# A ten-stage transformer block: norm roots moved to GpSimd, and the causal convolution as 128x32 products

## The chip, the cores and the metric

The kernel runs on one core of a Trainium2 chip. The metric is the time of one execution in microseconds (us) of device time, as a median over runs. The engines are TensorE (PE; its weight loads are listed apart as PEld), VectorE (DVE), ScalarE (ACT), GpSimd (POOL) and SyncE (SP), whose queue issues nearly all transfers here.

## The reference, cut to what matters

Batch 1, 256 rows, width 1024, float32. Ten stages follow each other on the same residual `x`: a gated feed-forward net (F1), a mixer with convolution and windowed attention ("even"), F3, F4, forgetting attention ("fox"), F6, an mLSTM mixer ("ml"), F8, attention with relative positions ("rel"), F10, and a last norm. Every stage begins with an RMS norm of `x`; the first six also norm their result before it is added.

```python
def _rmsnorm(x, g):
    y = x * rsqrt(mean(x * x, axis=-1) + EPS)
    return y * g

def _conv_module(u, gate, w, b, ln_g, ln_b):      # u, gate: (256, 512)
    a = u * sigmoid(gate)
    y[t, c] = sum(a[t - 30 + j, c] * w[j, c] for j in range(31)) + b[c]
    y = layernorm(y) * ln_g + ln_b
    return silu(y)

h = concat([_conv_module(...), window_attention(...)]) @ w_out     # the even mixer
x = x + _rmsnorm(h, g3)
```

## The kernel before, in words

The 256 rows are two blocks of 128, b0 and b1. Every large product runs in the reduced type fp32r three times: each operand is split into a high part `hi` (an ACT copy) and a low part `lo` (a DVE subtraction), and `mm3` (line 673) adds hi·hi, hi·lo and lo·hi. The weights come as "units" of 128 x 2048 (two transfers of 512 KB), are split into tiles `hl`, and are used by both blocks. So the bulk of DVE's work are subtractions `hl<-b,hl` (`tt`, line 220, recorded as L223), the bulk of ACT's are copies `hl<-b` (L213), and the bulk of PE's are products of 512 columns (`mm`, line 280, recorded as L293; transposes are L298).

The order of the work is not that of the code. Every helper only records an operation with an engine, an estimated duration and a key (where in the sequence of units it belongs; block b1 lies `lead` = 4 units behind b0). `schedule` (line 319) then plays the engines' queues through with these estimates and hands out the buffers, and the instructions are emitted in the order of the starts that it finds. A table NUDGE (line 1732) shifts the keys of some 970 labelled groups by fixed amounts. Each engine then runs its own queue in order.

**The norms' roots.** `rstd` (line 579) takes sums of squares that ACT left in a column and makes 1/sqrt by VectorE alone: a first guess from the bits, three Newton steps, all on tiles `s` of 128x1 (or 128x4 for the mLSTM heads). For a norm at the start of a stage (`norm`, line 662, which also wants halves of the root) these are 12 instructions, for one at the end (`postnorm`, line 714) 10. `postnorm` squares the two halves of the result by ACT, multiplies them by the gain (DVE, L242 `b<-acc,g`), takes the root, and updates `x` (DVE, L242 `x<-b,s,x`); the next stage's `gain_T` (line 634) then multiplies `x` by the next gain (DVE, L223 `b<-x,g`) and transposes (L298). There are 20 roots at starts, 12 at ends, 2 in the convolution's layernorm, 4 for the mLSTM heads. The last norm (`final`, line 1620) alone already takes its root by GpSimd (`pow`, line 267): one TENSOR_SCALAR (L271) and one TENSOR_TENSOR with power -1/2 (L273).

**The convolution** (`even`, line 1260). The gated input is transposed to channels x time (four tiles `ct` of 128 channels; tile `aT`, with 30 zero columns ahead). Of the 4 x 31 taps, `cg` = 6 groups of 8 go to TensorE: all 31 taps of ct 0 and 15 of ct 1, for each block a product with a 128x128 diagonal matrix that is loaded (`in_diag`), 2 x 46 = 92 products of 128 columns in full float32. The trace shows a float32 product as two matmuls:

```python
for q in range(4 - ng[ct], 4):
    n = min(8, 31 - 8 * q)
    d = r.t("b4", n * P, name="diag")
    r.load(d[:, :], self.a["diag"][ct][:, q * 1024:q * 1024 + n * P], ...)
    for j in range(n):
        r.mm(bank[:, 0:P], d[:, j * P:(j + 1) * P], tap(ct, b * P + 8 * q + j, P), ...)
```

The other 78 taps run on VectorE, each one multiply-add over 128x256 (L242 `b<-aT,cst,b`). Then follow the layernorm, its transposes and the silu; in the output projection the convolution's channels come last (`order=(2, 3, 0, 1)`).

Buffers: `b4` (nine of 128x1024; raw weights, `y`, the diagonals, scores), `b2` (eleven of 128x512), `s` (sixteen), `aT` (four), and four PSUM banks `mm` and four `acc`.

Of the kernel before, what the change touches and what calls it, by code (L numbers as in the profile page):

```python
# [12 lines left out]
P = 128  # L13
# [63 lines left out]
class Rec:  # L77
# [13 lines left out]
    def alloc(self, ctx):  # L91
        for tag, (dt, cols, n, psum) in self.tags.items():
            kw = dict(space=(None, bass.MemoryType.PSUM, bass.MemoryType.DRAM)[psum]) if psum else {}
            pool = ctx.enter_context(self.tc.tile_pool(name="p_" + tag, bufs=1, **kw))
            rows = 16 if psum == 2 else P
            self.phys[tag] = [pool.tile([rows, cols], dt, tag=f"{tag}{i}", name=f"{tag}{i}") for i in range(n)]
# [170 lines left out]
    def pow(self, s, a, b, key=None):  # L267

        v, y, e = s[:, 0:1], s[:, 1:2], s[:, 2:3]
        self.op("POOL", 350, [a, b], [v],  # L270
                lambda: self.nc.gpsimd.tensor_scalar(self.res(v), self.res(a), self.res(b), EPS, ALU.add, ALU.add), key=key)  # L271
        self.op("POOL", 600, [v, e], [y],
                lambda: self.nc.gpsimd.tensor_tensor(self.res(y), self.res(v), self.res(e), ALU.pow), key=key)  # L273
        return y
# [25 lines left out]
    def load(self, out, src, nbytes, key=None, after=None):  # L300
        o = self.op("DMA", max(nbytes / (360.0 if key > 0 else 250.0), 453.0), [src], [out],
# [187 lines left out]
class Net:  # L489
# [12 lines left out]
    def consts(self):  # L502
# [3 lines left out]
        w = r.t("s", name="warm")  # L506
        r.memset(w[:, 0:1], 0.0, key=-40)
# [6 lines left out]
        for b in range(2):  # L514
            x = r.t("x", name=f"x{b}")
            for h in range(2):
                r.load(x[:, h * 512:(h + 1) * 512], a["x"][b * P:(b + 1) * P, h * 512:(h + 1) * 512], P * 2048, key=-30 + 0.15 * b + 0.75 * h)
# [61 lines left out]
    def rstd(self, ss, w, n, key, more=False, cut=1):  # L579
# [3 lines left out]
        v, vh, y, t = s[:, 0:w], s[:, w:2 * w], s[:, 2 * w:3 * w], s[:, 3 * w:4 * w]  # L583
        r.begin()
        r.ts(v, ss[0], 1.0 / n, EPS, ALU.mult, ALU.add)
        if len(ss) > 1:
            r.end(key)
            r.begin()
            r.stt(v, ss[1], 1.0 / n, v, ALU.mult, ALU.add)
        r.ts(y.bitcast(I32), v.bitcast(I32), -0.5, 1597463007.0, ALU.mult, ALU.add)  # L590
        r.ts(vh, v, -0.5, None, ALU.mult)
        for i in range(3):
            if w == 1:
                r.stt(t, y, vh, y, ALU.mult, ALU.mult)
            else:
                r.tt(t, y, y, ALU.mult)
                r.tt(t, t, vh, ALU.mult)
            r.stt(y, t, 1.5, y, ALU.add, ALU.mult)
            if cut > 1 and i < 2:
                r.end(key)  # L600
                r.begin()
        if more:
            r.stt(s[:, 5:6], y, 0.5, y, ALU.mult, ALU.mult)
            r.ts(s[:, 4:5], y, 0.5, None, ALU.mult)
        r.end(key)
        if more:
            return y, s[:, 4:5], s[:, 5:6]
# [17 lines left out]
    def ssq(self, b, key):  # L625
# [3 lines left out]
        for h in range(2):  # L629
            junk = r.t("b2", name="junk")  # L630
            r.act(junk[:, :], self.x[b][:, h * 512:(h + 1) * 512], AF.Square, accum=ss[:, h:h + 1], key=key)
# [82 lines left out]
    def postnorm(self, b, acc, g, scale):  # L714
# [5 lines left out]
        for h in range(2):  # L720
            sl = slice(h * 512, h * 512 + 512)
            junk = r.t("b2", name="junk")
            r.act(junk[:, :], acc[h][:, :], AF.Square, accum=ss[:, h:h + 1], key=key)
# [185 lines left out]
    def attn_group(self, b, key, qT, kT, v, bias, sgn, O, oc, den, sink=None, nd=2):  # L909
# [5 lines left out]
        sc = r.t("b4" if nk == 2 else "b2", name="sc")  # L915
# [146 lines left out]
    def fox(self, gi):  # L1062
# [51 lines left out]
        for b in range(2):  # L1114
            den.append(r.t("s", name="den"))
            vv[b] = r.t("b4", name="v")
        for j in range(4):
            for b in range(2):
# [15 lines left out]
                C = r.t("b4" if b else "b2", name="C")  # L1134
# [33 lines left out]
    def rel(self):  # L1168
# [19 lines left out]
        for b in range(2):  # L1188
# [15 lines left out]
            vv[b] = r.t("b4", name="v")  # L1204
# [55 lines left out]
    def even(self, gi):  # L1260
# [12 lines left out]
        cw, cbi, lg, lb = c[:, 520:644], c[:, 644:648], c[:, 648:652], c[:, 652:656]  # L1273
# [3 lines left out]
        T2 = 30 + 2 * P  # L1277
        a2 = [r.t("aT", 2 * T2, name="aT") for _ in range(2)]
        y = r.t("b4", name="yT")
        ng = [min(4, max(0, int(self.c["cg"]) - 4 * ct)) for ct in range(4)]  # L1280
        part = [None, None]

        def tap(ct, t0, n):
            o = (ct % 2) * T2 + t0
            return a2[ct // 2][:, o:o + n]

        for b in range(2):
# [14 lines left out]
            for i in range(2):  # L1302
                if b == 0:
                    r.begin()
                    for ct in (2 * i, 2 * i + 1):
                        r.memset(tap(ct, 0, 30), 0.0)
                    r.end(key)
                r.begin()
                for ct in (2 * i, 2 * i + 1):
                    r.copy(tap(ct, 30 + b * P, P), pt[:, ct * P:(ct + 1) * P])  # L1310
                r.end(key)
            r.lab = f"even conv b{b}"
            kp = self.pos(b, u0 + 3) - self.c["vp"]
            for ct in range(4):
                if ng[ct] == 0:
                    continue
                bank = r.t("mm", name="cv")
                for q in range(4 - ng[ct], 4):
                    n = min(8, 31 - 8 * q)
                    d = r.t("b4", n * P, name="diag")  # L1320
                    at = u0 + self.c["lead"] * b + self.c["du"] + 4 * ct + q
                    r.load(d[:, :], self.a["diag"][ct][:, q * 1024:q * 1024 + n * P], P * P * 4 * n, key=at, after=self.near(at))
                    r.begin()
                    for j in range(n):
                        r.mm(bank[:, 0:P], d[:, j * P:(j + 1) * P], tap(ct, b * P + 8 * q + j, P), q == 4 - ng[ct] and j == 0, q == 3 and j == n - 1)
                    r.end(kp)
                ys = y[:, (2 * ct + b) * P:(2 * ct + b + 1) * P]
                if ng[ct] == 4:
                    r.act(ys, bank[:, 0:P], AF.Identity, bias=cbi[:, ct:ct + 1], key=kp)
                else:  # L1330
                    part[b] = r.t("b1", name="part")
                    r.act(part[b][:, 0:P], bank[:, 0:P], AF.Copy, key=kp)
        r.lab = "even conv"
        key = self.pos(1, u0 + 3) - self.c["vb"]
        for j in range(31):
            r.begin()
            for ct in range(3, -1, -1):
                if j >= 8 * (4 - ng[ct]):
                    continue
                ys = y[:, 2 * ct * P:2 * (ct + 1) * P]  # L1340
                w = cw[:, ct * 31 + j:ct * 31 + j + 1]
                if j == 0:
                    r.ts(ys, tap(ct, j, 2 * P), w, cbi[:, ct:ct + 1], ALU.mult, ALU.add)
                else:
                    r.stt(ys, tap(ct, j, 2 * P), w, ys, ALU.mult, ALU.add)
            r.end(key)
        for ct in range(4):
            if 0 < ng[ct] < 4:
                for b in range(2):
                    ys = y[:, (2 * ct + b) * P:(2 * ct + b + 1) * P]  # L1350
                    r.tt(ys, part[b][:, 0:P], ys, ALU.add, key=key)
# [586 lines left out]
```

## Time and profile before

| what | us |
|---|---|
| median of 3 runs (lowest, highest) | 1586.29 (1584.86, 1587.45) |
| the profiled execution | 1587.08 |
| its span, first to last instruction | 1585.3 |
| TensorE busy | 1548.6 |
| VectorE busy | 1217.4 |
| ScalarE busy | 938.1 |
| GpSimd busy | 1.9 |

A group's row reads: line, engine, operation, out<-in by the program's names (buffer numbers left out), shapes, count | busy us, mean ns of one | idle time of the engine just before them and what ended it. In a timeline a row begins with the start and the duration of a run of like instructions. Matmuls overlap each other in the array, so the pace of a stream is read from starts, not from the mean of one.

### The profile page before, as it was taken

How to read it: one execution, taken by the hardware profiler on the slowest of the kernel's cores; microseconds unless marked ns; L12 is line 12 of the kernel's file. 1: busy time of each engine (PE TensorE's matmuls, PEld its weight loads, DVE VectorE, ACT ScalarE, POOL GpSimd, SP SyncE). 2: the span in 40 equal slices, each digit the busy share in tenths (PEclk: the TensorE clock that was granted, in tenths of full speed). 3: DMA queues.
4: the chain of work that ended last, by engine and by line, in shares of the span. 5: the costliest groups of instructions: out<-in, count | busy, mean ns of one | idle time of the engine just before them, and what ended most of it. 6: DMA issues, size and time to landing. Idle time of an engine off the chain costs nothing.

```text
span 1585.3 us, 21242 instructions
## 1 busy us (share of the span) xinstructions
PE 1548.6 (98%) x7546; PEld 1266.6 (80%) x7546; DVE 1217.4 (77%) x2137; ACT 938.1 (59%) x1480; POOL 1.9 (0%) x8
## 2 busy tenths in 40 slices
PE   8999999999999999999999999999999999999998
PEld 6888878788887888787787887788877887788886
DVE  6555689798878869776899687898788674788784
ACT  6444545865555656456875565656566566765562
POOL 0000000000000000000000000000000000000000
PEclk9999999999999999999999999999999999999999
DMA  8556466447474475643664475455463755464560
GB/s 329 199 186 210 164 219 222 136 169 232 146 269 156 152 242 166 223 155 125 208 207 166 168 259 196 130 184 188 158 212 134 245 174 178 165 216 149 188 231 35
DMA packets 86779, 296.92 MB, mean 187 GB/s; under 512 B 9552, under 2 KB 13072, under 8 KB 86672
## 3 DMA queue, kind: packets, MB, share of 16 engines
q1 hardware_dynamic: 86384, 295.03, 55.1%
q8 instruction: 59, 0.97, 0.2%
q10 hardware_dynamic: 288, 0.52, 0.1%
q14 instruction: 48, 0.39, 0.1%
HBM read 294.44 MB, written 1.08 MB: 186 GB/s over the span
## 4 chain that ended last, share of the span: by engine, by line
PE 90%; DVE 6%; ACT 1%; issue 1%; DMA 1%; SPq 0%; POOLq 0%; POOL 0%; DVEq 0%; ACTq 0%
PE mm L293 59%; PE acc L293 27%; PE mm L298 4%; DVE hl L223 1%; DVE b L242 1%; DVE s L242 1%; ACT b L213 1%; DVE b L223 1%; DMA b<-in_w 1%; DVE x L242 1%; DMA x<-in_x 0%; DVE xt L223 0%; DVE s L233 0%; DVE b L254 0%; ACT L213 0%
## 5 line engine op out<-in xcount | busy, mean ns | idle before, releaser
L293 PE MATMUL mm<-hl,xt 128*128 128x512 f32 (+1 forms) x4104 | 983.6, 393 | 5.6 <-DVE xt L223 1.9
L293 PEld LDWEIGHTS mm<-hl,xt 128*128 128x128 f32 x4104 | 758.1, 188 | 168.7 <-DVE xt L223 4.8
L223 DVE TENSOR_TENSOR hl<-b,hl 128x1024 fp32r<-128x1024 f32 (+1 forms) x554 | 660.7, 1212 | 147.5 <-PE mm L293 70.5
L213 ACT ACTIVATE hl<-b 128x1024 fp32r<-128x1024 f32 (+1 forms) x554 | 572.5, 1052 | 325.4 <-PE mm L293 196.3
L293 PE MATMUL acc<-hl,gt 128*128 128x512 f32 x1584 | 385.7, 393 | 1.2 <-DVE gt L223 0.7
L293 PEld LDWEIGHTS acc<-hl,gt 128*128 128x128 f32 x1584 | 296.8, 189 | 63.9 <-DVE gt L223 1.9
L213 ACT ACTIVATE b<-mm,s 128x256 f32<-128x256 f32 (+2 forms) x150 | 77.3, 520 | 157.6 <-PE mm L293 151.1
L223 DVE TENSOR_TENSOR b<-b,b 128x1024 f32<-128x1024 f32 (+2 forms) x112 | 116.8, 1057 | 10.9 <-DMA b<-in_w 10.1
L298 PE MATMUL mm<-cst,b 128*128 128x128 f32 (+1 forms) x648 | 96.2, 276 | 9.7 <-DVE b L223 4.3
L298 PEld LDWEIGHTS mm<-cst,b 128*128 128x128 f32 (+1 forms) x648 | 77.5, 141 | 32.7 <-DVE b L223 7.0
L242 DVE SCALAR_TENSOR_TENSOR b<-mm,s,b 128x256 f32<-128x256 f32 x102 | 48.9, 479 | 63.2 <-ACT b L213 62.9
L293 PE MATMUL acc<-hl,xt 128*128 128x512 f32 x384 | 93.2, 395 | 0.9 <-DVE hl L223 0.9
L213 ACT ACTIVATE b<-b,s 128x256 f32<-128x256 f32 (+2 forms) x184 | 77.8, 450 | 24.9 <-DVE b L223 14.9
L293 PEld LDWEIGHTS acc<-hl,xt 128*128 128x128 f32 x384 | 70.6, 188 | 17.3 <-DVE hl L223 1.3
L223 DVE TENSOR_TENSOR gt<-mm,gt 128x512 fp32r<-128x512 f32 (+1 forms) x72 | 46.1, 642 | 32.7 <-ACT gt L213 32.4
L213 ACT ACTIVATE gt<-mm 128x512 fp32r<-128x512 f32 (+1 forms) x72 | 39.7, 553 | 41.7 <-PE mm L298 37.8
L213 ACT ACTIVATE b<-mm 128x512 f32<-128x512 f32 (+3 forms) x84 | 45.2, 546 | 13.8 <-PE mm L298 10.7
L242 DVE SCALAR_TENSOR_TENSOR s<-s 128x1 f32<-128x1 f32 (+2 forms) x248 | 45.4, 183 | 7.4
L213 ACT ACTIVATE b<-x 128x512 f32<-128x512 f32 x44 | 27.5, 627 | 25.8 <-DVE x L223 12.4
L242 DVE SCALAR_TENSOR_TENSOR hl<-b,cst,hl 128x512 fp32r<-128x512 f32 x48 | 33.1, 745 | 7.7 <-issue 7.6
L213 ACT ACTIVATE hl<-b,cst 128x512 fp32r<-128x512 f32 x48 | 32.7, 719 | 4.1 <-PE mm L293 3.3
L213 ACT ACTIVATE xt<-mm 128x512 fp32r<-128x512 f32 x40 | 23.4, 593 | 15.8 <-PE mm L298 14.9
(79 smaller groups left out, 597.9 us busy)
## 6 DMA issues: line engine op xcount, KB each, us to landing
b<-in_w SPq DMA_DIRECT2D x512, 512.0 KB, 5.1
g<-in_gains SPq DMA_DIRECT2D x16, 512.0 KB, 6.8
b<-in_diag SPq DMA_DIRECT2D x8, 512.0 KB, 4.6
b<-dr SPq DMA_DIRECT2D x16, 256.0 KB, 5.7
g<-in_relb SPq DMA_DIRECT2D x4, 512.0 KB, 4.7
b<-in_diag SPq DMA_DIRECT2D x4, 448.0 KB, 7.9
x<-in_x SPq DMA_DIRECT2D x4, 256.0 KB, 2.8
b<-in_w SPq DMA_DIRECT2D x4, 256.0 KB, 6.0
```

The source lines that it names most:

```text
L213: return self.nc.scalar.activation(self.res(out), self.res(in_), func, **kw)
L223: lambda: self.nc.vector.tensor_tensor(self.res(out), self.res(a), self.res(b), op), key=key)
L242: lambda: self.nc.vector.scalar_tensor_tensor(self.res(out), self.res(a), self.res(s), self.res(b), op0, op1, **kw), key=key)
L293: lambda: self.nc.tensor.matmul(self.res(out), self.res(l), self.res(r), start=start, stop=stop, **(dict(skip_group_check=True) if again e ...
L298: lambda: self.nc.tensor.transpose(self.res(out), self.res(in_), self.res(ident)), key=key)
```

## The change

1. `rstd` runs on GpSimd everywhere: one TENSOR_SCALAR (sum of the two halves plus EPS; the squares are scaled by 1/32 before), one TENSOR_TENSOR with power -1/2, and for a norm at the start a third one for the half. All VectorE instructions of the root go.
2. The convolution runs on TensorE alone. ACT copies the transposed input with one instruction a block, SP stores it to a DRAM tile `da` (512 channels x 288), and for each ct four loads bring it back as four copies shifted by 0 to 3 columns, 32 channels on 32 partitions each. A product then takes 4 taps of 32 channels: 128 rows, 32 output columns, 256 time columns at once; 8 x 4 x 4 = 128 products, going round the four groups of 32 output partitions. Their weights (`cw`) are one load of 512 KB a ct.
3. The order is made anew: all of NUDGE, the order of the first loads of `x` (both halves of b0 first), the estimates for loads, GpSimd and the new products. `b2` goes from 11 to 10 buffers, `s` from 16 to 14, `b4` tiles are 1152 wide.

```diff
 def rstd(...)
-        r.begin()
-        r.ts(v, ss[0], 1.0 / n, EPS, ALU.mult, ALU.add)
+        v, y = s[:, 0:w], s[:, w:2 * w]
         if len(ss) > 1:
...
-        for i in range(3):
-            if w == 1:
-                r.stt(t, y, vh, y, ALU.mult, ALU.mult)
...
+            r.pts(v, ss[0], ss[1], EPS, ALU.add, ALU.add, key=key)
+        else:
+            r.pts(v, ss[0], 1.0 / n, EPS, ALU.mult, ALU.add, key=key)
+        r.ptt(y, v, self.mhalf[:, 0:w], ALU.pow, key=key)
         if more:
...
+            r.pts(s[:, 2 * w:2 * w + 1], y, 0.5, None, ALU.mult, key=key)
 def mm(...)
+        elif ls[1] == 32:
+            d = 115.0
 def consts(...)
-                r.load(x[...], ..., key=-30 + 0.15 * b + 0.75 * h)
+                r.load(x[...], ..., key=-30 + self.c["xb"] * b + 0.2 * h)
 def even(...)
+            r.copy(av[:, :, 30 + b * P:30 + b * P + P], pt[:, :].rearrange("p (c t) -> p c t", c=4), key=key)
+            t0 = 0 if b == 0 else 30 + P
+            r.store(dv[:, :, t0:30 + P + b * (P + 2)], av[:, :, t0:30 + P + b * (P + 2)], ..., key=key)
+        for ct in range(4):
+            kp = self.pos(1, u0 + 3) - self.c["vp"] + 2 * ct
+            w, B = r.t("b4", 1024, name="cw"), r.t("b4", 4 * 284, name="taps")
+            r.load(w[:, :], self.a["cw"][ct], P * 4096, key=kp - 2, after=self.near(kp - 2))
+            B3 = B[:, :].rearrange("p (g t) -> p g t", g=4)
+            for q in range(4):
+                r.load(B3[32 * q:32 * q + 32], da[P * ct:P * ct + P, q:q + 284].rearrange("(g c) t -> c g t", g=4), 128 * 284 * 4, key=kp)
+            bank = r.t("mm", name="cv")
+            for m in range(8):
+                for g in range(4):
+                    o = g * 284 + 4 * m
+                    r.mm(bank[32 * g:32 * g + 32, 0:256], w[:, (4 * m + g) * 32:(4 * m + g + 1) * 32], B[:, o:o + 256], m == 0, m == 7)
+            r.act(y[:, 256 * ct:256 * ct + 256], bank[:, 0:256], AF.Identity, bias=cbi[:, ct:ct + 1], key=kp)
```

## Rows read from the trace of the kernel before

**Rows 1.** The page, part 1: span, busy time, share and instructions of each engine.

```profile
span 1585.3 us, 21242 instructions
PE 1548.6 (98%) x7546; PEld 1266.6 (80%) x7546; DVE 1217.4 (77%) x2137; ACT 938.1 (59%) x1480; POOL 1.9 (0%) x8
```

**Rows 2.** Stretches: length, then busy us (instructions) by engine, granted clock, DMA share, GB/s.

```profile
46.00:195.00 149.00, 149.00 (x677) 123.19 (x675) 80.47 (x96) 71.41 (x89) 0.00 (x0) 1.00 0.57 192
195.00:305.00 110.00, 103.93 (x651) 87.48 (x650) 96.29 (x253) 69.42 (x155) 0.00 (x0) 1.00 0.58 195
650.00:700.00 50.00, 46.29 (x223) 37.75 (x222) 36.59 (x89) 26.49 (x44) 0.00 (x0) 0.93 0.38 130
```

**Rows 3.** Waits of PE: for whom, us in total, times, longest.

```profile
PE mm L298 <- DMA x<-in_x: 7.0, 2, 4.0
PE mm L298 <- DVE b L223: 4.3, 3, 2.0
PE mm L298 <- DVE b L242: 4.2, 4, 2.2
```

**Rows 4.** Timeline of the even stage, 222 to 292 us: copies of `aT`, diagonal and narrow products.

```profile
227.55 0.79 ACT L213 ACTIVATE aT<-mm 128x128 f32<-128x128 f32 x4 [1.02 <-PE mm L298]
...
256.32 3.84 PE L293 MATMUL mm<-aT,b 128*128 128x128 f32 x32
...
260.00 0.60 PE L298 MATMUL mm<-cst,b 128*128 128x128 f32 x4
...
265.69 1.09 PE L293 MATMUL acc<-b,b 128*64 128x128 f32 x16
...
266.71 1.65 PE L293 MATMUL acc<-hl,xt 128*128 128x512 f32 x6
```

**Rows 5.** Groups by shape: the convolution's products, its VectorE taps, and the splits.

```profile
L293 PE MATMUL mm<-aT,b 128*128 128x128 f32 x184 | 22.2, 277 | 0.0
L242 DVE SCALAR_TENSOR_TENSOR b<-aT,cst,b 128x256 f32<-128x256 f32 x75 | 31.1, 475 | 0.0
L223 DVE TENSOR_TENSOR hl<-b,hl 128x1024 fp32r<-128x1024 f32 x548 | 657.5, 1219 | 146.7 <-PE mm L293 70.5 <-ACT hl L213 31.1 <-PE acc L293 29.5
```

**Rows 6.** Transfers: KB each, median us from issue to landing.

```profile
b<-in_diag SPq DMA_DIRECT2D x8, 512.0 KB, 4.6
b<-dr SPq DMA_DIRECT2D x16, 256.0 KB, 5.7
```

**Rows 7.** Groups by shape: the largest groups of the roots on VectorE.

```profile
L242 DVE SCALAR_TENSOR_TENSOR s<-s 128x1 f32<-128x1 f32 x224 | 41.5, 185 | 6.7
L233 DVE TENSOR_SCALAR s<-s 128x1 f32<-128x1 f32 x88 | 12.6, 145 | 0.0
```

**Rows 8.** Timeline of the boundary from F4 to fox, 655 to 680 us.

```profile
668.56 0.15 DVE L242 SCALAR_TENSOR_TENSOR s<-s,s 128x1 f32<-128x1 f32 x1
...
668.99 1.31 DVE L242 SCALAR_TENSOR_TENSOR s<-s 128x1 f32<-128x1 f32 x6
...
670.23 0.48 DVE L242 SCALAR_TENSOR_TENSOR b<-mm,s,b 128x256 f32<-128x256 f32 x1
670.63 1.40 DVE L242 SCALAR_TENSOR_TENSOR x<-b,s,x 128x512 f32<-128x512 f32 x2
...
670.77 0.44 PE L298 MATMUL mm<-cst,b 128*128 128x128 f32 x2 [2.22 <-DVE b L242]
...
672.69 1.97 PE L298 MATMUL mm<-cst,b 128*128 128x128 f32 x8 [1.49 <-DVE b L223]
```

**Rows 9.** Timeline of the last norm, 1570 to 1586 us: the root by GpSimd.

```profile
1574.08 0.19 ACT L213 ACTIVATION_READ_ACCUMULATOR b<-x 128x1 f32 x1
1574.37 0.30 POOL L271 TENSOR_SCALAR s<-s 128x1 f32<-128x1 f32 x1 [1573.94 <-ACT b L213]
1574.75 0.57 POOL L273 TENSOR_TENSOR s<-s 128x1 f32<-128x1 f32 x1
1575.36 0.72 ACT L213 ACTIVATE b<-b,s 128x512 f32<-128x512 f32 x1 [1.08 <-POOL s L273]
```

More of the change, by code (lines that the diff above doesn't have):

```diff
@@ L94, in alloc @@
             pool = ctx.enter_context(self.tc.tile_pool(name="p_" + tag, bufs=1, **kw))
-            rows = 16 if psum == 2 else P
+            rows = {"dr": 16, "da": 512}.get(tag, P)
             self.phys[tag] = [pool.tile([rows, cols], dt, tag=f"{tag}{i}", name=f"{tag}{i}") for i in range(n)]
@@ L300, in load @@
     def load(self, out, src, nbytes, key=None, after=None):
-        o = self.op("DMA", max(nbytes / (360.0 if key > 0 else 250.0), 453.0), [src], [out],
+        o = self.op("DMA", max(nbytes / 360.0 + 0, 453.0), [src], [out],
                     lambda: self.nc.sync.dma_start(self.res(out), self.res(src)),
@@ L506, in consts @@
         w = r.t("s", name="warm")
+        self.mhalf = r.t("s", name="mhalf")
+        r.memset(self.mhalf[:, 0:4], -0.5, key=-39)
         r.memset(w[:, 0:1], 0.0, key=-40)
@@ L582, in rstd @@
         s = r.t("s", name="rs")
[L583 to L585 removed]
+        v, y = s[:, 0:w], s[:, w:2 * w]
         if len(ss) > 1:
[L587 to L591, printed above, removed]
[L592 to L607 removed]
+            r.pts(v, ss[0], ss[1], EPS, ALU.add, ALU.add, key=key)
+        else:
+            r.pts(v, ss[0], 1.0 / n, EPS, ALU.mult, ALU.add, key=key)
+        r.ptt(y, v, self.mhalf[:, 0:w], ALU.pow, key=key)
+        if more:
+            r.pts(s[:, 2 * w:2 * w + 1], y, 0.5, None, ALU.mult, key=key)
+            return y, s[:, 2 * w:2 * w + 1]
         return y
@@ L914, in attn_group @@
         first = len(r.ops)
-        sc = r.t("b4" if nk == 2 else "b2", name="sc")
+        sc = r.t("b4" if nk == 2 else "b2", 512 * nk, name="sc")
         S = [r.t("mm", name="S") for _ in range(2)]
@@ L1133, in fox @@
                 r.lab = f"fox bias{j} b{b}"
-                C = r.t("b4" if b else "b2", name="C")
+                C = r.t("b4" if b else "b2", 512 * (b + 1), name="C")
                 for kb in range(b + 1):
@@ L1276, in even @@
         kv, oT = [None] * 2, [None] * 2
[L1277 to L1285, printed above, removed]
+        T2 = 32 + 2 * P
+        aT = r.t("b4", 4 * T2, name="aT")
+        av = aT[:, :].rearrange("p (c t) -> p c t", c=4)
+        da = r.t("da", name="da")
+        dv = da[:, :].rearrange("(c p) t -> p c t", c=4)
+        y = r.t("b4", 1024, name="yT")
         for b in range(2):
@@ L1301, in even @@
             r.end(key)
[L1302 to L1332, printed above, removed]
@@ L1333, in even @@
-        r.lab = "even conv"
-        key = self.pos(1, u0 + 3) - self.c["vb"]
-        for j in range(31):
-            r.begin()
[L1337 to L1351, printed above, removed]
+            if b == 0:
+                r.memset(av[:, :, 0:30], 0.0, key=key)
+                r.memset(av[:, :, 30 + 2 * P:], 0.0, key=key)
+            r.copy(av[:, :, 30 + b * P:30 + b * P + P], pt[:, :].rearrange("p (c t) -> p c t", c=4), key=key)
+            t0 = 0 if b == 0 else 30 + P
```

60 lines of the change are left out of this document (32 added, 28 removed), and 306 rows, old and new, of the table NUDGE.

## The prediction

> **What bounds the kernel now.** I read the busy shares first [rows 1]. TensorE is busy 1548.6 of 1585.3 us, VectorE 77%. So all that can be had without touching TensorE's own work is what it stands idle, 36.7 us, and the rest must come out of its products. The stretches say where that idle time lies [rows 2]: inside a feed-forward net there is none (149.00 of 149.00 us busy), in the even stage with the boundary ahead of it 6.1 us of 110, around the boundary from F4 to fox 3.7 us of 50, with a granted clock of 0.93 instead of 1.00. TensorE's waits name the sources [rows 3]: the first loads of `x` (7.0 us), and VectorE's tiles at the transposes that open a new stage (4.3 and 4.2 us in seven waits). One of these boundaries in order of time shows the mechanism [rows 8]: the root's instructions begin at 668.56 us, the update of `x` comes at 670.63; in between, VectorE is not free for the tile at 670.23 that TensorE needs, and it stands still for 2.22 us, then for 1.49 us more until `x` is updated and multiplied. A measurement of this kernel can tell about 0.2%, some 3.2 us, from no change.
>
> **Part 1, the convolution's products.** Before: 184 matmuls, 92 products [rows 5]. Their pace by starts is 32 in 3.68 us (256.32 to 260.00), 115 ns each, so 230 ns a product and 21.2 us in all [rows 4]. After: 128 products of 256 columns. No such product is in the trace. The nearest row is that of products with 64 output columns, which go round two groups of output partitions: 16 matmuls in 1.02 us (265.69 to 266.71), 64 ns each, 128 ns a product of 128 columns [rows 4]. At full width that would be 230, so two groups do run together, at 1.8 times the pace. With twice the columns and four groups instead of two, the same 128 ns: 16.4 us, a gain of 4.8. Bounds: four groups without any loss, 460/4 = 115 ns, 14.7 us, gain 6.5; two at a time as in the row, 256 ns, 32.8 us, a loss of 11.6; none together, 460 ns, 58.9 us, a loss of 37.7. I take 128, as the same row shows that narrow products overlap; the two losses stay as a rival.
>
> The Trainium skill, TensorE: Matmul & The Clock Gate, section Measured speedup vs the span model, gives 2.38 times for three column tiles of 32. That is 0.79 a tile where the row here gives 0.9 for two; by it, an estimate, a product would take some 145 ns and the gain be 2.6 us.
>
> **Part 2, VectorE's taps.** 75 multiply-adds of 31.1 us in all go [rows 5], out of a stage in which VectorE is busy 96.3 of 110 us, the tightest of the stretches read [rows 2]. TensorE's 6.1 us of idle time there hang partly on the boundary (part 4), partly on attention work that stands between the taps in VectorE's queue. I take 2 us of it; bounds 0 and 4.
>
> **Part 3, the way through DRAM.** It puts two stores and sixteen loads, besides four of weights, into SP's queue, in place of twelve loads of diagonals. They move fewer bytes. A transfer out of DRAM of 256 KB in rows lands 5.7 us after its issue at the median [rows 6]; store and load one after the other are then some 11 us from the copy of `aT`, which ended at 228.3 [rows 4], to the first product at about 240. The old products still ran at 256 to 260, and q, k, v and the attention are there to cover. So I put it at nothing. If the cover is gone it costs up to those 11 us, and since SP issues in order, the unit loads behind the waiting store are late by its landing as well: the splits `hl` wait for them first, TensorE after that. `b4` holds the taps too, so fewer raw weights are ahead. ACT gets fewer, wider copies: nothing. The layernorm behind the convolution keeps its chain.
>
> **Part 4, the roots.** The two largest groups alone take 54.1 us from VectorE [rows 7]. Most of that was hidden: TensorE was working for the other block. What counts is the chain at a stage's end. By VectorE it takes 2.07 us (668.56 to 670.63) [rows 8]. By GpSimd the last norm shows it: 0.30 and 0.57 us of work, and 0.99 us from its start at 1574.37 to the reader's at 1575.36 [rows 9]. That is 1.1 us shorter, in each of the seven waits of [rows 3], 7.7 us at the most; together they last 8.5. But a wait that becomes shorter at one tile uncovers the next (the 1.49 us behind the 2.22 in [rows 8] depends on ACT's squares and on the gain product too), so I take a third, 2.5 us. GpSimd's queue holds nothing else, so nothing is held up behind it. In the last norm GpSimd is already in use: nothing. If the boundaries' stalls shorten, TensorE's clock falls less: 0.07 of 50 us is 3.5 us at most [rows 2]; I take 0.5.
>
> The last norm's row has no VectorE work beside GpSimd's. Against other work the price is open: bounds are 0.99 us, and both GpSimd instructions held for one split of 1219 ns each [rows 5], 3.43 us, which is 1.36 longer than by VectorE; seven times that is a loss of 9.5. I take the measured 0.99 and keep the loss for a rival.
>
> The Trainium skill, SBUF — State Buffer, section Who interferes with whom, speaks against this change: a VectorE instruction with two inputs in SBUF and a GpSimd instruction that reads SBUF lock each other out for a whole instruction. The splits `hl<-b,hl` have two such inputs. No row here shows the two side by side; by the rule the gain of this part would be none or negative.
>
> **Part 5, the start and the order.** Both halves of b0's `x` come ahead of b1's. Of the 7.0 us that TensorE waited for `x`, the longer wait is 4.0 [rows 3]; that is the bound to either side, since the later block's rows now come later. I take 0.5. The order made anew can shift every small stall; I put it at nothing, with 4 us to either side for the range. One buffer less of `b2` and two of `s`: nothing, since with the roots the longest-lived scratch columns go too.
>
> **The sum.** 4.8 + 2 + 2.5 + 0.5 + 0.5 = 10.3 us less. The profiled execution took 1587.08 (span 1585.3 and 1.8 around it), so 1576.8; it lies 0.8 above the median of the runs shown, so **1576.0** for a median.
>
> **The rivals.**
> - *More comes back.* The seven waits lose their full 1.1 us, the even stage its 4 us, the clock 2 us: 6.5 + 4 + 7.7 + 2, some 20 us less, about 1566. For it: a whole chain of small instructions leaves a queue that TensorE waits for. Against it: each removed wait has a successor.
> - *Only the products.* The roots and taps were hidden, as 149.00 of 149.00 us elsewhere suggests; 4.8 us and a little are left: 1581.
> - *GpSimd behind the splits.* Its two instructions wait for a VectorE split each, as priced above: 4.8 + 2 gained, 9.5 lost, 1589 with the other terms at nothing; with half of it 1584. Within 0.2%.
> - *Slower: the column groups do not run four at once.* Place: the 128 narrow products. Two at a time they cost 32.8 us, 16.4 more than forecast: 1592. One at a time 58.9: 1618. The break-even with all else as forecast lies at 10.3 us more than 16.4, 26.7 us, 209 ns a product. Against it: the two-group row runs at 1.8 times the pace.
>
> **How the numbers follow.** Forecast 0.52 (its own range 1570 to 1583), more 0.17, only the products 0.15, GpSimd behind the splits 0.07, slower by the column groups 0.06, slower by late copies through DRAM or the new order 0.03. Faster by over 0.2% is below 1583.1: the first three, 0.84. Same: the fourth, 0.07. Slower: 0.09. The range of 8 in 10 leaves out half of "more" and the slower cases: 1564 to 1587.
>
> **What would show it.** Right: 256 matmuls of 128 rows and 32 columns whose starts lie about 64 ns apart; VectorE some 85 to 105 us less busy and below 75% in the even stage; the waits of the transposes for VectorE below 5 us; roots by GpSimd about 1 us from sum to reader. Wrong: matmuls 128 ns apart or more (part 1), GpSimd rows much longer than 0.30 and 0.57 us beside splits (part 4), TensorE waiting for the taps' loads or for late units in the even stage (part 3), or new waits in stages that the change does not touch (the order).

## The result, and the profile after

| | before | after |
|---|---|---|
| median of the runs shown, us | 1586.29 | 1569.80 |
| profiled execution, us (its span) | 1587.08 (1585.3) | 1569.8 (1568.0) |
| mean granted clock of TensorE | 0.997 | 0.996 |

The ratio is 0.990, with a 95% interval of 0.988 to 0.992: 16.5 us less, where 10.3 were forecast. The time lies inside the range; the way to it does not follow the sum, so that the time came out near is in part luck.

First the busy shares of the kernel after, which answer to [rows 1].

```profile
span 1568.0 us, 21032 instructions
...
PE 1535.4 (98%) x7618; PEld 1256.2 (80%) x7618; DVE 1135.6 (72%) x1628; ACT 938.2 (60%) x1474; POOL 66.6 (4%) x104
```

VectorE is 82 us less busy. TensorE's idle time (span less busy) fell from 36.7 to 32.6 us only; the other 13.2 us came out of its busy time, of which the convolution's products explain 6.0 (22.2 in [rows 5], and 9.06 + 7.11 below). The rest may be time that "busy" hides: an f32 transpose counts as busy for 275 ns, though eight in a row take 1.04 us (a row of c2 below), so a wait of a tenth of a microsecond behind one appears nowhere as idle. No row shows that this makes up the whole rest. Starts, not busy sums, show such time.

The stages show where it went. The table has, from the timeline's rows of VectorE, the start of the last update of `x` in a stage, in us; the last three columns are experiments that are told of below (old order with roots by GpSimd; searched orders for the old kernel, and for the old convolution with roots by GpSimd).

| stage | before | after | a1 | c1 | c2 |
|---|---|---|---|---|---|
| F1 | 206.8 | 203.1 | 202.8 | 207.0 | 201.4 |
| even (convolution) | 308.5 | 303.4 | 308.6 | 308.3 | 298.0 |
| F3 | 496.6 | 486.6 | 497.5 | 498.1 | 487.1 |
| F4 | 683.9 | 672.0 | 682.6 | 682.9 | 669.5 |
| fox | 805.8 | 793.8 | 803.6 | 806.0 | 787.9 |
| F6 | 993.3 | 975.7 | 990.4 | 990.5 | 971.3 |
| F10 | 1578.3 | 1561.1 | 1576.3 | 1576.1 | 1557.7 |

The even stage, the only one with a convolution, takes 101.7 us before (308.5 - 206.8) and 100.3 after: 1.4 us of the 17.2 in the last row. F1, F3 and F6, which the convolution does not touch, give 3.7, 4.9 and 5.6. Behind the mLSTM mixer, whose last update of `x` starts at 1101.7 before and at 1082.0 after, nothing came back: F8, rel and F10 together take 476.6 us before and 479.1 after. Their roots stand at the starts of stages only.

Why the even stage gave so little: its stretches, by windows, in the columns of [rows 2] (the first line answers to the line of the same window there).

```profile
195.00:305.00 110.00, 103.47 (x749) 81.57 (x748) 61.48 (x117) 73.96 (x158) 11.58 (x19) 0.97 0.66 197
239.30:250.80 11.50, 8.02 (x60) 6.39 (x61) 6.35 (x28) 7.11 (x18) 0.00 (x0) 0.88 1.05 226
250.80:259.80 9.00, 8.99 (x129) 5.05 (x129) 2.19 (x16) 6.08 (x25) 0.00 (x0) 0.78 0.75 214
259.80:270.00 10.20, 10.20 (x165) 6.50 (x161) 2.73 (x13) 7.87 (x22) 0.00 (x0) 1.00 0.43 128
```

VectorE is at 56% in place of 88%, as meant. But TensorE still stands idle for 6.5 of 110 us (6.1 before), and the granted clock is 0.97 in place of 1.00. The timeline of TensorE in that stretch, with the new products (128x32, moving 256 columns):

```profile
239.33 0.66 PE L304 MATMUL mm<-cst,b 128*128 128x128 f32 x4 [2.74 <-ACT b L213]
...
247.22 1.38 PE L299 MATMUL mm<-b,b 64*128 64x256 f32 x8 [0.97 <-DVE b L260]
250.81 9.06 PE L299 MATMUL mm<-b,b 128*32 128x256 f32 x128 [2.21 <-DMA b<-da]
...
262.90 7.11 PE L299 MATMUL mm<-b,b 128*32 128x256 f32 x128
```

Three stalls, together 5.9 us, stand ahead of the products. Then the first half of them takes 9.06 us at a granted clock of 0.78, the second 7.11 at 1.00. The second is the products' true pace: 256 matmuls would be 14.2 us, 55 ns each and 111 ns a product, so four groups of output columns do run at once (b1 below has the products one by one). The first stall begins in SP's queue, ahead of the store:

```profile
221.80 0.93 SPq L308 DMA_DIRECT2D g<-in_gains  x1
226.42 0.38 SPq L322 DMA_DIRECT2D da<-b  x1
...
227.44 1.12 SPq L308 DMA_DIRECT2D b<-in_w  x2
231.70 0.81 SPq L308 DMA_DIRECT2D b<-da  x2
232.60 0.86 SPq L308 DMA_DIRECT2D b<-in_w  x2
```

From 222.73 to 226.42 SP issues nothing: the store waits for the copy that ACT makes for it, and two pieces of a weight unit stand behind it, at 227.44. The chain of releases in order of time (start, duration, what) goes on from there; the row of ACT is from the timeline:

```profile
225.79 0.61 ACT b L213
...
227.44 7.81 DMA b<-in_w
...
235.27 11.02 DMA b<-da
...
246.30 4.23 DMA b<-da
...
250.81 9.06 PE mm L299 x128
```

```profile
235.34 1.06 ACT L213 ACTIVATE hl<-b 128x1024 fp32r<-128x1024 f32 x1 [3.36 <-DMA b<-in_w]
```

The first piece lands 7.81 us after its issue, where 5.1 is the median over the kernel. ACT's split waits 3.36 us for it, a copy that TensorE's transposes need stands behind that split on ACT, and the 2.74 us are the result. The first loads of the copies follow the store by 5.3 us, at 231.70 (such a store lands 5.2 us after its issue by the view of the DMAs); the pieces issued behind them, at 232.60, are not the ones that ACT waited for. The copies themselves are slow: one load out of DRAM takes 11.02 us, another 4.23, and the products start at 250.81. In all this time the DMA engines are full (the last two columns, share and GB/s):

```profile
223.00:232.00 9.00, 9.00 (x44) 7.42 (x43) 5.01 (x5) 3.68 (x5) 0.00 (x0) 1.00 0.99 335
232.00:239.30 7.30, 4.60 (x31) 4.00 (x29) 1.79 (x2) 3.18 (x4) 0.00 (x0) 1.00 1.02 264
```

With 239.30:250.80 above, the share is 0.99, 1.02 and 1.05; in the same three windows before it was 0.91, 0.37 and 0.36.

What TensorE waits for in the whole kernel after (us in total, times, longest), against [rows 3]:

```profile
PE mm L304 <- DMA x<-in_x: 7.6, 3, 4.4
PE mm L304 <- DVE b L223: 3.7, 2, 3.4
PE mm L304 <- ACT b L213: 2.9, 2, 2.7
PE mm L299 <- DMA b<-da: 2.2, 1, 2.2
PE mm L304 <- DVE b L242: 2.1, 2, 1.2
```

The transposes' waits for VectorE (`b`, lines L223 and L242) went from 8.5 us to 5.8. One of 3.4 us is still there.

### The profile page after: what moved, and what is told of

The parts are those of the page before. It is cut to its first block, busy times and chain, and to the rows that moved or that the text cites. A ratio compares the mean times of both kernels' runs of the same rounds, so it can differ in the third digit from the quotient of the medians.

```text
span 1568.0 us, 21032 instructions
## 1 busy us (share of the span) xinstructions
PE 1535.4 (98%) x7618; PEld 1256.2 (80%) x7618; DVE 1135.6 (72%) x1628; ACT 938.2 (60%) x1474; POOL 66.6 (4%) x104
## 4 chain that ended last, share of the span: by engine, by line
PE 75%; issue 18%; DMA 3%; DVE 2%; ACT 1%; POOL 0%; SPq 0%; POOLq 0%; DVEq 0%; ACTq 0%
PE mm L299 48%; PE acc L299 23%; PE mm L304 4%; DMA b<-in_w 2%; DMA b<-da 1%; DVE hl L223 1%; ACT b L213 1%; ACT hl L213 1%; DMA x<-in_x 0%; DVE b L223 0%; POOL s L272 0%; DVE b L242 0%; POOL s L278 0%; SPq L308 0%; ACT xt L213 0%
## 5 line engine op out<-in xcount | busy, mean ns | idle before, releaser
L223 DVE TENSOR_TENSOR hl<-b,hl 128x1024 fp32r<-128x1024 f32 (+2 forms) x554 | 661.1, 1214 | 182.1 <-PE mm L299 63.3
L213 ACT ACTIVATE hl<-b 128x1024 fp32r<-128x1024 f32 (+2 forms) x554 | 573.0, 1054 | 331.9 <-PE mm L299 184.1
L299 PE MATMUL acc<-hl,gt 128*128 128x512 f32 x1584 | 380.3, 391 | 0.0
L223 DVE TENSOR_TENSOR b<-b,b 128x1024 f32<-128x1024 f32 (+1 forms) x110 | 116.6, 1074 | 12.5 <-DMA b<-in_w 10.7
L272 POOL TENSOR_SCALAR s<-s 128x1 f32<-128x1 f32 (+1 forms) x60 | 37.6, 627 | 1493.4 <-ACT b L213 1419.3
L213 ACT ACTIVATE b<-b,s 128x128 f32<-128x128 f32 (+2 forms) x184 | 77.8, 449 | 38.2 <-DVE b L223 23.1
L242 DVE SCALAR_TENSOR_TENSOR b<-mm,s,b 128x256 f32<-128x256 f32 x102 | 48.9, 480 | 66.9 <-ACT b L213 66.5
L223 DVE TENSOR_TENSOR gt<-mm,gt 128x512 fp32r<-128x512 f32 (+1 forms) x72 | 46.1, 643 | 29.4 <-ACT gt L213 28.9
L242 DVE SCALAR_TENSOR_TENSOR hl<-b,cst,hl 128x512 fp32r<-128x512 f32 x48 | 33.3, 747 | 16.5 <-issue 9.0
L299 PE MATMUL mm<-b,b 128*32 128x256 f32 (+2 forms) x464 | 39.1, 381 | 3.3 <-DMA b<-da 2.2
L299 PEld LDWEIGHTS mm<-b,b 128*32 128x32 f32 (+1 forms) x464 | 24.8, 150 | 17.7 <-issue 5.2
```

What stands on the lines that cost most here:

```text
L213: return self.nc.scalar.activation(self.res(out), self.res(in_), func, **kw)
L223: lambda: self.nc.vector.tensor_tensor(self.res(out), self.res(a), self.res(b), op), key=key)
L242: lambda: self.nc.vector.scalar_tensor_tensor(self.res(out), self.res(a), self.res(s), self.res(b), op0, op1, **kw), key=key)
L272: return self.nc.gpsimd.tensor_scalar(*args)
L299: lambda: self.nc.tensor.matmul(self.res(out), self.res(l), self.res(r), start=start, stop=stop, **(dict(skip_group_check=True) if again e ...
```

## The experiments

Medians of one kernel differ by some 2 us between chips, so each run is compared, by its ratio, with the kernel before, run beside it on the same chip; "against after" is that ratio over 0.990, which is itself known to some 3 us either way.

### Each part alone, first without a searched order

**a1: roots by GpSimd in the old order.** Each instruction of the kernel before stays at its place; the chain on VectorE becomes three on GpSimd.

```diff
+                g.tensor_scalar(f(v), f(ss[0]), f(ss[1]), EPS, ALU.add, ALU.add)
...
+            k = g.tensor_tensor(f(y), f(v), r.phys["mh"][0][:, 0:w], ALU.pow)
...
+        for o in r.ops[n0:]:
+            o.em = []
+        r.ops[-1].em = [power]
```

> The kernel before, its order of work kept instruction by instruction, with the roots of all the norms done by GpSimd (add, power) in place of VectorE's chain of some ten small instructions. Theory (the roots carry most of what came back: the traces show the stages without convolution, F3, F6 and ml, some 14 us shorter together): 6 to 12 us less than before, and VectorE some 50 us less busy. Rival 1 (the order made anew carries it, the roots were hidden): within 2 us of before. Rival 2 (GpSimd is held by VectorE's splits, as in the row of 3.62 us): up to 9 us slower.

Measured: 1585.33 us, ratio 0.9975 (0.9966 to 0.9985), that is 4.0 us less by the ratio (2.4 to 5.4; 3.1 by the two medians); VectorE 1164.1 us busy, 53 less. Theory and both rivals miss. In the table above F1 is 4.0 us shorter, and the even stage takes as much longer. The boundary from F4 to fox, as in [rows 8], shows why so little comes back.

```profile
668.40 0.30 POOL L612 TENSOR_SCALAR s<-s 128x1 f32<-128x1 f32 x1 [167.52 <-ACT b L213]
668.78 0.57 POOL L615 TENSOR_TENSOR s<-s,mh 128x1 f32<-128x1 f32 x1
668.98 1.06 ACT L213 ACTIVATE hl<-b 128x1024 fp32r<-128x1024 f32 x1 [0.67 <-PE mm L293]
669.94 0.46 ACT L213 ACTIVATE b<-mm,s 128x256 f32<-128x256 f32 x1
670.43 0.48 DVE L242 SCALAR_TENSOR_TENSOR b<-mm,s,b 128x256 f32<-128x256 f32 x1 [1.40 <-ACT b L213]
670.83 1.41 DVE L242 SCALAR_TENSOR_TENSOR x<-b,s,x 128x512 f32<-128x512 f32 x2
...
670.97 0.44 PE L298 MATMUL mm<-cst,b 128*128 128x128 f32 x2 [2.03 <-DVE b L242]
```

The root is ready at 669.35. But the update of `x` that reads it starts at 670.83, no earlier than before (670.63 there): ahead of it in VectorE's queue stands a multiplication that waits for ACT, and ACT does a split first. VectorE is idle for 1.40 us in just the time that was freed. At this boundary the old order cannot use it. The kernel before has the same copy by ACT:

```profile
669.55 0.46 ACT L213 ACTIVATE b<-mm,s 128x256 f32<-128x256 f32 x1
```

It ends at 670.01, so there the root's chain held the multiplication at 670.23 [rows 8] back by some 0.2 us, and not by TensorE's whole 2.22.

**a2: roots back on VectorE in the order of after.** **d1: GpSimd does the roots as in after, and VectorE runs its old chain besides,** into columns that nobody reads. **b2: GpSimd writes every power three times.** All three keep the order of after.

```diff
 a2, in rstd:
-        r.ptt(y, v, self.mhalf[:, 0:w], ALU.pow, key=key)
+        r.ops[-1].em = [newton]
 d1, in rstd:
+        r.ops[-1].em = [lambda: (pw(), idle_chain())[0]]
 b2, in ptt:
-                lambda: self.nc.gpsimd.tensor_tensor(self.res(out), self.res(a), self.res(b), op), key=key)
+                lambda: [self.nc.gpsimd.tensor_tensor(self.res(out), self.res(a), self.res(b), op) for _ in range(3)][-1], key=key)
```

> The kernel after, its order kept, with every norm's root put back on VectorE as the old chain of small instructions, at the place where GpSimd's power stood (the last norm's root too, which was GpSimd's already). Theory (roots are most of the gain): 8 to 14 us slower than after, most of it at the stage boundaries. Rival 1 (the order carries it): 0 to 3 us slower. An order made for short roots may also suffer more than the old order did, so this is the upper end of what the roots are worth and the run of the old order with GpSimd roots is the lower end.

> The kernel after, its order kept, with every root's power written three times in place of once by GpSimd (same inputs, same result), some 1.2 us more from sum to reader at each norm and nothing more for any other engine. Theory (the length of the chain from sum to update of the residual is on the path at the stages' ends, some twenty norms in pairs): 6 to 15 us slower than after. Rival (what counts is only that VectorE is rid of the chain's instructions; GpSimd's own time is hidden by the other block's work): within 3 us of after.

> The kernel after, its order kept, roots by GpSimd as in it, with VectorE made to run its old chain of some nine small instructions as well, at the same places, into scratch columns that nobody reads. The chain from sum to reader is as short as in after; only VectorE's time for the roots is back. With the powers written three times (1.2 us longer, VectorE as free as in after) the time was 10 to 12 us more, with the roots on VectorE 33 us more. Theory (what the roots cost is VectorE's time in its queue more than the length of their chain): 15 to 25 us slower than after, 1585 to 1597. Rival (the length of the chain is what costs, VectorE's instructions fit beside): within 5 us of after.

| run | time, us | ratio to before | against after |
|---|---|---|---|
| a2 | 1603.69 | 1.0091 (1.0075 to 1.0108) | 30 us more |
| b2 | 1581.76 | 0.9958 (0.9945 to 0.9971) | 9 us more |
| d1 | 1601.22 | 1.0076 (1.0059 to 1.0092) | 28 us more |

a2 costs more than twice the theory's upper end: in an order made for short roots, roots on VectorE are far dearer than the 16.5 us of the whole change. b2 bears the theory out: two powers more, 0.72 us each at the mean of that run's powers, are worth 9 us; VectorE's updates of `x` wait 13.4 us for GpSimd there, 0.6 in after. d1 says what the rest is; at 28 us it lies beyond its theory's 15 to 25. The expectation calls the chain in d1 as short as in after; that holds for the root, but its reader, the update of `x`, stands in VectorE's queue behind the idle chain. So d1 has the longer way and VectorE's lost time together, and reaches all of a2 but what the intervals cannot tell apart. About 9 of its 28 us are then the length, an estimate by b2, and the larger part is the time that VectorE's other tiles lose. Busy shares and the waits of TensorE in d1:

```profile
PE 1549.0 (97%) x7618; PEld 1260.3 (79%) x7618; DVE 1192.5 (75%) x2000; ACT 939.7 (59%) x1474; POOL 60.8 (4%) x104
...
PE mm L299 <- DVE xt L223: 11.0, 6, 3.0
PE mm L304 <- DVE b L223: 10.4, 8, 4.4
```

57 us more on an engine that is busy 75% of the time: TensorE now waits for `xt`, the low parts of the transposed activations, an instruction that reads no root (11.0 us; 1.7 in after). They are late because they queue behind the roots, as the boundary from F3 to F4 shows, where VectorE stands idle in none of the rows:

```profile
490.25 0.21 DVE L602 TENSOR_SCALAR s<-s 128x1 f32<-128x1 f32 x1
...
492.00 2.36 DVE L223 TENSOR_TENSOR hl<-b,hl 128x1024 fp32r<-128x1024 f32 x2
494.27 1.28 DVE L223 TENSOR_TENSOR xt<-mm,xt 128x512 fp32r<-128x512 f32 x2
...
495.01 2.50 PE L299 MATMUL mm<-hl,xt 128*128 128x512 f32 x5 [2.98 <-DVE xt L223]
```

The idle chain lies between 490.25 and 492.00. Of the 31.6 us that the span of d1 is longer, 18.0 are idle time of TensorE; its granted clock is 0.988 (0.996 in after). And the loss has a place: F8, rel and F10 together take 479.4 us (479.1 in after), though their roots are back on VectorE as well. All of it lies ahead of them, in the stages with roots at their ends and in the mLSTM mixer.

**a3: the new convolution alone; a4: the new roots with the old convolution.** Here the order is planned anew, but with a list of adjustments that was searched for another program: a3 takes that of before, a4 that of after.

```diff
 a3, against before:
+            for m in range(8):
+                for g in range(4):
+                    ...
+                    r.mm(bank[32 * g:32 * g + 32, 0:256], ...)
```

In a4, against after, the same lines are taken out, and the old loop over `q` and the taps are put back.

> The kernel before with the new convolution alone (128x32 products over copies made through DRAM), roots still on VectorE, the order planned anew with the old adjustments. Theory: the products give back 5 us, the copies through DRAM take 5 to 8 us (SP's queue stands behind the store, unit loads are late), so within 4 us of before. Rival (forecast of record: way through DRAM hidden, products and taps give 6.8 us): 1578 to 1581. A third possibility, since the order is planned anew without a new search: up to 10 us slower from stalls outside the even stage, which the stage ends of its trace would show.

> The kernel after with the old convolution (128x128 products of loaded diagonals and VectorE's taps), roots on GpSimd, order planned anew with the adjustments of after. Theory (the convolution's gain is nearly eaten by the way through DRAM): within 4 us of after. Rival (forecast of record: convolution worth 6.8 us): 5 to 8 us slower than after, with the difference inside the even stage. Stalls outside the even stage would be the new plan's and speak for neither.

The expectations' first choices fail: a3 took 1652.7 us, ratio 1.0400 (1.0379 to 1.0422); a4 1593.42, ratio 1.0029 (1.0016 to 1.0042). Neither says anything of its part. In a3 the even stage ends 11.5 us late (320.0), fox 47.4 (853.2), F6 64.3 (1057.6), though the convolution is in neither of the last two. A list that fits one program is nearly worthless for another, so the parts must be compared in orders that were searched for each.

### The parts with an order searched for each

Four kernels, each with its own list, searched with as many tries by the kernel's own planner: before, roots alone, convolution alone, both.

```diff
 NUDGE = {
-    ...
+    ...
 }
```

> The kernel before with nothing but its list of adjustments to the order searched further, some 12,000 tries by the kernel's own planner; the three runs beside it have their lists searched with as many tries. Theory (the roots by GpSimd carry most of the gain, once the order is made for them): a searched order alone gives 3 to 12 us, 1576 to 1585. Rival (the order alone carries the gain): within 4 us of after, 1566 to 1574.

> Roots by GpSimd with the old convolution, its order searched with as many tries as that of the kernel before beside it. Theory (the roots' gain comes out only where the order uses the freed VectorE): 10 to 20 us less than the searched kernel before beside it, so 1558 to 1572. Rival (forecast of record, roots 3 us; and 3.2 us as measured with the old order kept): 2 to 5 us less than it.

> The new convolution with the roots still on VectorE, its order searched with as many tries. Theory (products and taps give some 5 us, the way through DRAM takes as much): within 4 us of the searched kernel before beside it. Rival (forecast of record, the convolution is worth 6.8 us): 5 to 9 us less than it.

> The kernel after with its list of adjustments searched further with as many tries. Theory (parts add up: roots 10 to 20, convolution 0 to 8): 1552 to 1566, some 4 to 16 us less than after and 15 to 28 less than the searched kernel before beside it. Rival (the list of after is as good as the chip lets it be; a plan that looks better is not): within 3 us of after.

| | old convolution | new convolution |
|---|---|---|
| roots by VectorE | c1: 1582.81, 0.9964 (0.9951 to 0.9976) | c3: 1590.55, 1.0016 (1.0007 to 1.0026) |
| roots by GpSimd | c2: 1567.20, 0.9872 (0.9857 to 0.9887) | c4: 1563.10, 0.9842 (0.9828 to 0.9857) |

The theory's numbers hold for c1, c2 and c4; for c3 neither theory nor rival does. The order alone (c1) gives 5.8 us (1588.57 for the kernel before beside it, less 1582.81); it does not carry the change. The roots give 15.6 us with the old convolution (1582.81 - 1567.20) and 27.5 with the new one. (The lower row also has the new order of the first loads of `x` and the new estimates for them; that bears on the start, where TensorE waits 6.9 and 7.2 us for `x` in c2 and c4, 4.2 and 6.8 in c1 and c3, so it is not where the gain comes from.) The convolution costs 7.7 us alone and gives 4.1 with the roots. c2, with no new convolution at all, is no slower than the kernel after (0.9872 against 0.990, the intervals overlap by a little), and c4 is 9 us faster than it: the best of all.

How much of this is the luck of a search? The program of after in its own list and in c4's differs by 9 us, that of before in its own and in c1's by 6. So the roots' 15.6 and 27.5 stand in their sign, though not to the microsecond; the convolution's two numbers, of opposite sign, do not settle what it is worth over the whole kernel. In its own stage, from the end of F1 in one profiled execution each, the four take 101.3 (c1), 95.7 (c3, new convolution alone), 96.6 (c2, roots alone) and 95.4 us (c4). So the convolution alone gives 5.6 us where it stands, the roots alone 4.7, and the two hardly add. What c3 loses lies in F3 and F4, which have no convolution: 383.6 us together, 374.6 in c1.

The same boundary from F4 to fox in c2:

```profile
657.66 5.74 PE L297 MATMUL acc<-hl,gt 128*128 128x512 f32 x24
...
658.51 0.30 POOL L272 TENSOR_SCALAR s<-s 128x1 f32<-128x1 f32 x1 [168.35 <-ACT b L213]
658.89 0.57 POOL L278 TENSOR_TENSOR s<-s,s 128x1 f32<-128x1 f32 x1
...
660.52 1.41 DVE L242 SCALAR_TENSOR_TENSOR x<-b,s,x 128x512 f32<-128x512 f32 x2
...
663.24 1.04 PE L302 MATMUL mm<-cst,b 128*128 128x128 f32 x8
...
664.75 0.73 PE L297 MATMUL mm<-hl,xt 128*128 128x512 f32 x2 [0.47 <-ACT xt L213]
```

While root, update and gain go through, TensorE has 24 more products (5.74 us) and comes to the transposes at 663.24 without an idle bracket. In [rows 8] it stood still for 2.22 and 1.49 us at the same place. From GpSimd's start to the update it is 2.0 us (658.51 to 660.52), in a1 2.4 (668.40 to 670.83), by VectorE 2.07 [rows 8]: no shorter. What counts is the work that stands beside it. The group of all the transposes but the first, in c1 and then in c2 (busy, mean, idle ahead of them):

```profile
L298 PE MATMUL mm<-cst,b 128*128 128x128 f32 (+1 forms) x648 | 94.1, 275 | 8.5 <-DVE b L242 3.6 <-DVE b L223 2.9 <-ACT b L213 1.0
```

```profile
L302 PE MATMUL mm<-cst,b 128*128 128x128 f32 (+1 forms) x648 | 91.4, 273 | 2.6 <-DVE b L223 1.6 <-DVE b L242 0.9
```

### The convolution's own claims

**b1: the eight products of one column group after one another,** in place of going round the four groups.

```diff
-            for m in range(8):
-                for g in range(4):
+            for g in range(4):
+                for m in range(8):
```

> The kernel after, its order kept; only the two inner loops over a tile's 32 products change places, so that the eight products of one group of 32 output partitions follow one another instead of going round the four groups. Same products, same sums. Theory (it is the going round that lets four narrow products run at once, 110 ns each in the trace): products of one group run one behind the other, some 460 ns each, 128 of them 59 us instead of 16, so 35 to 43 us slower than after. Rival 1 (narrow products are quick whatever the order): within 2 us of after. Rival 2 (two overlap even so): 15 to 20 us slower.

Measured: 1596.94 us, ratio 1.0055 (1.0038 to 1.0071), 25 us more than after. TensorE's timeline of the two halves of these products, the second at full clock:

```profile
247.76 24.81 PE L299 MATMUL mm<-b,b 128*32 128x256 f32 x128 [1.60 <-DMA b<-in_cw]
...
275.61 21.98 PE L299 MATMUL mm<-b,b 128*32 128x256 f32 x128
```

The second half takes 21.98 us against 7.11 in after: the going round is what makes them overlap, as the theory said. Its size was off: a product of 256 columns standing alone costs 343 ns (2 x 21.98 / 128), not 460.

**b3: the sixteen loads of the copies from GpSimd's queue,** so that SP never waits for the store to land.

```diff
-                r.load(B3[32 * q:32 * q + 32], da[...], 128 * 284 * 4, key=kp)
+                o = r.load(B3[32 * q:32 * q + 32], da[...], 128 * 284 * 4, key=kp)
+                o.em = [lambda q=q, ct=ct, B3=B3: r.nc.gpsimd.dma_start(...)]
```

> The kernel after, its order kept, with the sixteen loads of the convolution's copies out of DRAM issued from GpSimd's queue in place of SP's, so that the loads of weight units behind them no longer wait for the store to land. Theory (the even stage's new stalls of 2.7, 1.0 and 2.2 us and the granted clock of 0.78 behind them come from SP standing behind the store): the wait for the weight unit goes, 2 to 6 us less than after, 1564 to 1568. Rival 1 (the stall is the landing of the copies themselves, not the queue): within 2 us of after, TensorE still waits for the copies. Rival 2 (issuing from GpSimd is slow, some 1 us each, and the roots stand behind it): 2 to 10 us slower, with GpSimd's rows longer in the even stage.

Measured: 1568.48 us, ratio 0.9876 (0.9861 to 0.9891), 4 us less than after, about the theory's size, but with overlapping intervals, so not told apart for sure. In the profile the wait of 2.74 us became 0.78 and the even stage ended 3.0 us earlier (1.3 of that F1 had already), but a wait ahead of the products stayed, now for VectorE's scores; these had waited for a load of `in_swab` that took 15.93 us, the second row, from the chain of releases:

```profile
236.12 0.66 PE L304 MATMUL mm<-cst,b 128*128 128x128 f32 x4 [0.78 <-ACT b L213]
...
247.51 9.41 PE L299 MATMUL mm<-b,b 128*32 128x256 f32 x128 [2.37 <-DVE s L254]
```

```profile
230.99 15.93 DMA b<-in_swab
```

So where the copies' loads are queued explains most of the first stall, not the second, which only changes the transfer that it waits for. How these loads, issued behind the two pieces of the weight unit, made them late is not shown; the rows show full DMA engines and no more. In c4 the order alone, with SP's queue as in after, leaves 0.36 us of waiting for the copies.

## Why the prediction was right, and where it was wrong

**The step that failed** is in part 5: "The order made anew can shift every small stall; I put it at nothing, with 4 us to either side for the range." The order is worth far more than that and cannot be priced apart from the parts: the same program (roots by GpSimd, old convolution) takes 1593.42 us in a list made for another program and 1567.20 in its own, and the convolution alone 1652.7 and 1590.55. The sum came near because two misses cancel: the even stage gave 1.4 us of the 6.8 forecast for products and taps, and the other stages gave 15.8 of 17.2, where 3.5 were forecast. Of the signs that the prediction named, VectorE is 82 us less busy (85 to 105 named) and the transposes wait 5.8 us for it (below 5 named), and three signs of being wrong came: long GpSimd rows, waits for the copies' loads, waits for late units. The other steps, one by one:

- *Part 1, the products: right.* Forecast 16.4 us, measured 9.06 + 7.11 = 16.2. At full clock it would be 14.2, a little below the best bound (14.7). The worst bound, 58.9 for none together, was too high: b1 took 24.81 and 21.98, 46.8 us. The Trainium skill, TensorE: Matmul & The Clock Gate, section Measured speedup vs the span model, gives 2.38 times for three tiles, 0.79 a tile. On the right base, 343 ns, that gives an estimate of 343 / (4 x 0.79) = 109 ns a product, and the rows show 111: the rule held, and the estimate of 145 ns went wrong by its base, a product priced as two of 128 columns.
- *Part 2 and part 3, taps and DRAM: wrong.* Products and taps were to give 6.8 us, the way through DRAM to cost nothing. The even stage gained 1.4. Since the products gave 5.0 of it (21.2 - 16.2), taps and DRAM together cost 3.6. The sentence on the lost cover named a part of the mechanism ("since SP issues in order, the unit loads behind the waiting store are late"), and the sum then left it out. What it had wrong is the time: store and load were to take 11 us, the first product to start at about 240; with the DMA engines full, one load of a copy alone took 11.02, and the product started at 250.81. In an order searched for it the convolution's 6.8 is nearly right in its stage: from the end of F1, c3 takes 95.7 us and c1 101.3. But c2, with the old taps, takes 96.6 (298.0 - 201.4), and c4, with both, 95.4 (298.5 - 203.1): the roots alone give most of the same relief.
- *Part 4, the roots: right for the old order, mis-sized for the new.* Forecast 2.5 + 0.5; a1 measures 4.0. With an order made for them they give 15.6 and more. The term priced a shorter chain in seven visible waits of TensorE. In [rows 8] the chain held the tile at 670.23 back by some 0.2 us, and with GpSimd the update came no sooner (2.0 us in c2, 2.4 in a1). The term left out what d1 shows, that the chain's 57 us in VectorE's queue delay other tiles there, `xt` above all.
- *The clock's 0.5: nothing.* 0.997 before, 0.996 after. Around the boundary from F4 to fox it rose from 0.93 to 0.97 in 50 us, in the even stage it fell from 1.00 to 0.97 in 110.
- *The start's 0.5: wrong sign, and small.* The wait for `x` is 7.6 us instead of 7.0, and the first product of 512 columns starts at 10.98 instead of 9.69.

**The rivals.** "More comes back" has nearly the right time, 1566, with the wrong account: the even stage gave less, not more, and the waits that [rows 3] shows did not vanish in after. "Only the products" is excluded by a1 and c2. "Slower: the column groups do not run four at once" is excluded by the 111 ns; b1 shows that it was a true danger, 25 us off by the order of two loops. "GpSimd behind the splits" exists, as one row of after shows beside VectorE's:

```profile
480.18 3.62 POOL L272 TENSOR_SCALAR s<-s 128x1 f32<-128x1 f32 x1 [3.62 <-ACT b L213]
...
480.15 3.49 DVE L223 TENSOR_TENSOR hl<-b,hl 128x1024 fp32r<-128x1024 f32 x3
```

An addition that takes 0.30 us alone [rows 9] takes 3.62, as long as a run of three splits. The Trainium skill, SBUF — State Buffer, section Who interferes with whom, says that the two lock each other out, and this trace agrees for GpSimd. For VectorE it shows no cost: its splits take 1221 ns at the mean, 1219 before. The rival's loss did not come: in a1, whose additions of this kind have a mean of 736 ns, the roots still give 4.0 us. What the lock takes from the gain was not measured.

**What stays open.** What the convolution is worth by itself over the whole kernel: alone it lost 7.7 us, with the roots it gave 4.1, and two searches of one program differ by 6 to 9. Why c3's order is slow in F3 and F4, and why the DMA engines are full while the copies are loaded.

## What to carry to other kernels

Where an order was searched for one program, a part tried in that order shows only what the old order can use of it, and a part tried in a foreign list shows nothing: compare parts in orders searched for each with the same effort. Work taken off an engine that is "hidden" at 75% can still be worth a quarter to a half of its length (15.6 and 27.5 us for 56 here), if what the busiest engine reads next goes through the same queue; it was worth nothing in the three stages behind the mLSTM mixer. A transfer that has to wait belongs where no load that others need is queued behind it. Its landing is to be priced from a stretch in which the DMA engines are as full as they will be: 11.02 us came here, where 5.7 was taken.

## What was not expected of the hardware

- Products with 32 output columns that go round the four groups of output partitions cost 111 ns for 256 columns of f32 at full clock; those of one group after one another cost 343. The overlap is 3.1 times, and it hangs on the order of issue alone.
- A GpSimd instruction on 128x1 was held for 3.62 us, through three VectorE subtractions that followed one another, and got in between none of them.
- The DMA engines were as full at 226 GB/s (share 1.05, while the copies were loaded) as at 335 GB/s (0.99) a few microseconds earlier. Whether the copies' short rows are the reason was not tested.
